# One shifted projection for q, k and v, and a token-ordered ring for transposed q and k

## The chip, the cores and the metric

The kernel runs on one core of a Trainium2 chip. The metric is the device time of one execution in microseconds, lower being better; the figure for the kernel before is the median of three runs. Traces come from a hardware profiler, one execution per trace. Engine names are those of the profile: PE multiplies matrices (PEld is its weight loading), DVE is the vector engine, ACT the scalar engine, POOL the GpSimd engine, SP the queue that issues all DMAs of this kernel.

## What is computed

One encoder block over 2048 tokens of width 1024, in float32: an RMS norm, one wide input projection, two attention mixers, SiLU and sigmoid gates, and two further projections. The change lies in the attention part:

```python
q = rms_norm(q.reshape(bsz, S, H, 64), gain) * scale      # per head, k likewise
# mixer A: 8 query heads on 2 key heads, |key - query| <= 128, with a sink logit
# mixer B: three groups of 8 heads, offsets dilation*j with |j| <= 64, dilation 1, 4, 16
logits = where(valid, q @ k.T + bias_table[t5_bucket(rel * dilation)], -1e30)
out = softmax(logits) @ v     # the three groups of B are then joined by their denominators
```

A dilation of d splits the tokens into d classes (token modulo d); each class of 2048/d tokens attends within itself. So dilation 1 has one class of 16 blocks of 128 tokens, dilation 4 has four classes of 4 blocks, dilation 16 has sixteen classes of one block.

## The kernel before

The input is normed, transposed and kept in SBUF as two fp16 halves, `XH` and `XL` (high part and remainder), features on partitions and tokens along the free axis, with the first 256 tokens repeated behind the last. A product in near-float32 precision is three fp16 products: high by high, high by low, low by high.

After a start of about 80 us the main stage projects and attends in 14 **units** (`UNITS`): two of kind A (4 query heads and one key head each) and twelve of kind B (2 heads of one dilation). Counted from 0, units 4, 7, 10 and 13 are of dilation 1, units 1, 5, 8 and 11 of dilation 4; these eight are called **shifted** (`un.shift`). Every unit has 16 blocks of 128 tokens, worked in 8 pairs (`class Pair`). From about 1400 us on come the merge gates, the branch projections and the output projection.

Steps of one pair, in order:

- `matmuls` (L651): 24 steps (8 feature chunks by 3 fp16 products) with the token block as weights and the weight columns streamed, into a PSUM tile `pj` of 384 columns (q, k, v).
- `evac_qk`, `v_hi`, `v_lo` (L670, L685, L691): out of PSUM. `v_ones` (L678) is a small POOL memset of a v tile.
- `square`, `stats`, `newton`, `scale`, `gain`, `hi`, `lo`, `swap`: the per-head norm and the split into fp16 halves `spl`. `newton` is twelve small POOL instructions (L270 to L273), `gain` POOL L722, `swap` POOL L737.
- `turn` (L745): one DMA transpose for each block from `spl` into a tile `kq` of 6 rows of 128 tokens (q heads, then k halves).

An `Item` is one query block with two heads. `logits` (L805) multiplies q against the keys, `maxima` adds the bias and takes the row maximum on DVE, `exps`, `hi`, `lo` make two fp16 halves of the probabilities, `turn` (L843) transposes them by DMA, `values` (L854) multiplies with v. In dilation-1 units two POOL steps join the three groups: `collect` (L989) and `products` (L1010).

In a shifted unit a query block of 128 tokens needs 64 tokens of keys on either side. So k and v are projected from token blocks shifted by 64 (block c holds tokens 128c-64 to 128c+63; block 0 wraps around), and the keys of query block i are the shifted blocks i and i+1. Before, q is projected from unshifted blocks: two accumulations for each token block, 24 matmuls of 128 columns (q) and 24 of 256 (k and v), each with its own weight load. `kq` tiles come from 6 rotating buffers, with 3 more (`kq0`) for block 0, which the last item needs again. Each segment of keys from one tile takes two matmuls of its own (`v` = 0, 1) for each head.

**What sets the order.** Nothing is scheduled by a planner. `at(t, f)` puts a step at a position t on a common clock whose unit is one pair; `until(t)` emits all steps due. `NORM`, `LAGS`, `LS` and others hold the offsets. The time of emission alone sets the place in each engine's queue, and each engine works its queue strictly in that order; a step that waits holds up all that stand behind it. The logits of a pair's first item stand 2.887 after the pair's begin (`LS`); `turn` stands 1.118 after the pair's last projection. `FILLS` lists pairs in which gate projections are streamed as well; units 10 and 13 have none.

Of the kernel before, what the change touches and what calls it, by code (L numbers as in the profile page):

```python
# [101 lines left out]
T_OUT = (0.1, 0.1, 1.431, 2.0)  # L102
FILLS = ((2, None, (2, 2, 4, 5)), (3, 0, (8, 9, 10, 12)), (4, 1, (17, 18, 20, 21)), (5, 2, (24, 25, 26, 28)), (6, 3, (32, 35, 37, 38)), (7, 4, (40, 41, 42, 44)), (9, 6, (57, 59, 60, 61)), (10, 7, (64, 65, 66, 68)), (11, 10, (88, 89, 90, 92)), (8, 13, (116, 116, 118, 118)))
XT_BUFS = 14
KQ_BUFS = 6
VT_BUFS = 10
PT_BUFS = 4
N_BIAS_A = 384
# [3 lines left out]
def block_kernel(tc, x, w_units, w_gate, w_mrg, w_brn, w_out, w_bra, gain, qkg, sink, bias_a, bias_b, b_merge, out):  # L112
# [514 lines left out]

        return min(t, NPAIR + 1 + DRAIN * (t - NPAIR - 1))

    def subset(X, g, r, c, aligned):  # L630
        o = 128 * c if aligned else (128 * c or S // DIL[g]) - 64
        return xclass((XH, XL)[X], g, r)[:, :, o:o + 128]

    class Pair:

# [6 lines left out]
        def matmuls(self, i):  # L642
            un, (r, c) = self.un, self.subsets[i]
            self.ps[i] = ps = pj_p.tile([128, 512], F32, name="pj")
            out = []
            for a, b, aligned in ((0, 128, True), (128, 384, False)) if un.shift else ((0, 384, True),):
                h, lo = subset(0, un.g, r, c, aligned), subset(1, un.g, r, c, aligned)
                k = 0
                for ch in range(NCH):
                    for lhs, rhs in ((h, un.wh), (h, un.wl), (lo, un.wh)):  # L650
                        out.append(lambda lhs=lhs, rhs=rhs, ch=ch, a=a, b=b, k=k: T.matmul(  # L651
                            ps[:, a:b], lhsT=lhs[:, ch, :], rhs=rhs[:, ch, a:b], start=(k == 0), stop=(k == 23)))
                        k += 1
            return out

        def plan(self, e):
# [80 lines left out]
                G.tensor_copy(sp[:, i, nh:, :, :], sp[:, i, nq:nh, ::-1, :])  # L737

        def turn(self):
            for i, s in enumerate(self.subsets):  # L740
                if self.un.shift and s[1] == 0:
                    kq = wk.tile([128, 6, 128], F16, name="kq0", bufs=3)
                else:
                    kq = wk.tile([128, 6, 128], F16, name="kq", bufs=KQ_BUFS)
                nc.sync.dma_start_transpose(out=kq[:], in_=self.sp[:, i].rearrange("p a b c -> p (a b c)"))  # L745
                self.un.kq[s] = kq


    class Item:
        def __init__(self, un, r, i, h0):  # L750
            self.un, self.r, self.i, self.h0 = un, r, i, h0
            n = un.n
            self.p0 = 0
            if un.kind == "A":
                cs = [c for c in (i - 1, i, i + 1) if 0 <= c < n]
                self.keys = [((0, c), 0, 128) for c in cs]
                self.b0 = 128 * (cs[0] - i + 1)
            elif n == 1:
                cs = [0]
                self.keys = [((r, 0), 0, 128)]  # L760
                self.b0 = 64
            else:
                cs = [i, (i + 1) % n]
                self.keys = [((r, i), 0 if i else 64, 128), ((r, (i + 1) % n), 0, 128 if i + 1 < n else 64)]
# [24 lines left out]

        def logits(self):  # L790
            un = self.un
            q = un.kq[(self.r, self.i)]
            if un.kind == "A":
                self.sv = [s_p.tile([128, 512], F32, name="s")[:, :self.W] for _ in range(2)]
            else:
# [2 lines left out]
            for j in range(2):  # L798
                h = self.h0 + j
                kh = 0 if un.kind == "A" else h  # L800
                o = 0
                for s, k0, k1 in self.keys:
                    kt = un.kq[s]
                    for v in range(2):
                        T.matmul(self.sv[j][:, o:o + k1 - k0], lhsT=q[:, h, :],  # L805
                                 rhs=kt[:, un.nq + kh + v * un.nk, k0:k1], start=(v == 0), stop=(v == 1))
                    o += k1 - k0

# [938 lines left out]
```

## Time and profile before

| | us |
|---|---|
| median of 3 runs (lowest, highest) | 1958.43 (1956.13, 1965.45) |
| span of the profiled execution, first to last instruction | 1958.6 |
| busy in the span: PE, DVE, ACT, POOL | 1935.7, 1377.4, 1059.8, 956.0 |
| 0 to 80 us: PE busy | 71.1 of 80 |
| 80 to 480, 480 to 880, 880 to 1280 us: PE busy of 400 | 399.5, 397.0, 396.1 |
| 1400 to 1958 us: PE busy of 558 | 554.0 |

The profile gives no time of the profiled execution other than its span, which is 0.2 us from the median.

How to read what follows: an engine's row of busy time adds up the union of its instructions. Matmuls overlap each other in the record, so what a matmul costs in a stream is the distance between two starts, not its length. In the list of waits a row names who waited, for whom, how long in total, how often, and the longest. In the timeline a row has start, length, engine, line, operation and tiles; the idle time before it stands in brackets if there was any.

### The profile page before, as it was taken

The numbers are of one execution on the slowest core, as the hardware profiler recorded it, in microseconds if no ns is written. First come the engines' busy times: TensorE is split into PE (matmuls) and PEld (weight loads), VectorE is DVE, ScalarE is ACT, GpSimd is POOL, SyncE is SP. The second block draws the span as 40 slices with busy tenths as digits, with TensorE's granted clock in tenths as the row PEclk, the third lists the DMA queues.
The fourth block names the chain that finished last, engine by engine and source line by source line (L and its number), as shares of the span: only waits on it lengthen the run. The fifth ranks groups of instructions, "written<-read, shape, count | busy, mean of one in ns | idle before, by whom it ended". The sixth has DMA issues, their size and how long they took to land.

```text
span 1958.6 us, 48091 instructions
## 1 busy us (share of the span) xinstructions
PE 1935.7 (99%) x17606; PEld 1392.0 (71%) x17606; DVE 1377.4 (70%) x3604; ACT 1059.8 (54%) x2415; POOL 956.0 (49%) x2440
## 2 busy tenths in 40 slices
PE   8999999999999999999999999999999999999999
PEld 5567896677788898888989889899544444444444
DVE  6668777888768776667876878767776757876312
ACT  7457656776565566565666655656534545432100
POOL 4254556455546656647566676656511210232533
PEclk8999999999999999999999999999999999999999
DMA  6239987797848596677777776755822346788763
GB/s 250 81 81 168 194 150 159 141 187 141 177 101 184 118 185 126 125 148 164 152 132 154 135 169 126 143 118 118 187 81 85 106 165 195 218 241 268 252 228 145
DMA packets 589773, 308.46 MB, mean 157 GB/s; under 512 B 458080, under 2 KB 527328, under 8 KB 588256
## 3 DMA queue, kind: packets, MB, share of 16 engines
q1 hardware_dynamic: 589536, 305.39, 67.0%
q8 instruction: 137, 2.24, 0.5%
q14 instruction: 100, 0.82, 0.1%
HBM read 129.91 MB, written 65.27 MB: 100 GB/s over the span
## 4 chain that ended last, share of the span: by engine, by line
PE 80%; DVE 6%; POOL 6%; issue 4%; ACT 2%; DMA 2%; SPq 0%; POOLq 0%; DVEq 0%; ACTq 0%
PE pj L651 32%; PE pj L308 14%; PE fps L308 13%; PE fps L1614 7%; PE fps L1409 5%; PE s L805 4%; PE pv L854 4%; POOL rs_t L270 1%; DVE rw L715 1%; POOL rs_t L271 1%; DVE qss L703 1%; POOL rs_t L272 1%; POOL rw L722 1%; POOL rs_y L273 1%; PE pt L916 1%
## 5 line engine op out<-in xcount | busy, mean ns | idle before, releaser
L651 PE MATMUL pj<-wl,XH 128*128 128x128 f16 (+2 forms) x2816 | 715.2, 268 | 0.0
L651 PE MATMUL pj<-wh,XH 128*128 128x128 f16 (+2 forms) x2816 | 708.7, 268 | 4.0 <-DVE vt L691 4.0
L651 PE MATMUL pj<-wh,XL 128*128 128x128 f16 (+2 forms) x2816 | 711.6, 269 | 0.0
L651 PEld LDWEIGHTS <-XH 128*128 128x128 f16 x5632 | 574.6, 113 | 64.7 <-issue 5.8
L651 PEld LDWEIGHTS <-XL 128*128 128x128 f16 x2816 | 318.1, 113 | 26.7 <-issue 0.5
L820 DVE CUSTOM_DVE_ANT_0 pr<-s,b,ubuf 128x256 f32<-128x256 f32 (+3 forms) x512 | 218.6, 464 | 48.6 <-PE s L805 47.0
L270 POOL TENSOR_TENSOR rs_t<-rs_y 128x8 f32<-128x8 f32 (+2 forms) x345 | 105.4, 306 | 207.5 <-DVE rs_y L261 142.7
L837 DVE SCALAR_TENSOR_TENSOR p<-pr,p 128x512 f16<-128x512 f32 (+2 forms) x256 | 185.0, 723 | 21.6 <-ACT p L833 21.1
L308 PEld LDWEIGHTS <-wh 128*128 128x128 f16 x960 | 93.7, 98 | 111.0 <-issue 1.5
L715 DVE TENSOR_TENSOR rw<-rw,qr 128x512 f32<-128x512 f32 (+1 forms) x112 | 111.6, 997 | 86.7 <-POOL vt L678 58.4
L722 POOL TENSOR_TENSOR rw<-rw,g 128x128 f32<-128x128 f32 (+1 forms) x224 | 131.1, 605 | 78.1 <-DVE rw L715 62.1
L833 ACT ACTIVATE p<-pr 128x512 f16<-128x512 f32 (+2 forms) x256 | 159.5, 623 | 7.1 <-issue 0.3
L670 ACT ACTIVATE rw<-pj 128x256 f32<-128x256 f32 (+1 forms) x224 | 86.5, 386 | 134.3 <-PE pj L651 133.4
L737 POOL COPY spl<-spl 128x256 f16<-128x256 f16 (+1 forms) x224 | 93.7, 448 | 127.2 <-DVE spl L732 125.7
L308 PE MATMUL fps<-Y,wh 128*128 128x512 f16 x512 | 152.2, 379 | 0.0
L805 PE MATMUL s<-kq 128*128 128x128 f16 (+1 forms) x1856 | 147.3, 218 | 1.5 <-DMA kq<-spl 1.4
L805 PEld LDWEIGHTS <-kq 128*128 128x128 f16 x2016 | 129.8, 98 | 25.1 <-issue 2.0
L308 PE MATMUL pj<-XH,gh 128*128 128x512 f16 x384 | 145.5, 379 | 0.0
L308 PE MATMUL pj<-XH,gl 128*128 128x512 f16 x384 | 145.5, 379 | 0.0
L308 PE MATMUL pj<-XL,gh 128*128 128x512 f16 x384 | 145.5, 379 | 0.0
L1614 PE MATMUL fps<-wt,M 128*128 128x512 f16 (+1 forms) x684 | 145.2, 375 | 0.0
L728 ACT ACTIVATE spl<-rw 128x512 f16<-128x512 f32 (+1 forms) x112 | 72.1, 644 | 126.2 <-POOL vt L678 87.0
(241 smaller groups left out, 3702.2 us busy)
## 6 DMA issues: line engine op xcount, KB each, us to landing
wraw<-in_w_units_dram SPq DMA_DIRECT2D x56, 384.0 KB, 4.6
mtd<-mm SPq DMA_DIRECT2D x56, 256.0 KB, 3.7
M<-mtd SPq DMA_DIRECT2D x8, 1792.0 KB, 9.5
mgd<-fg SPq DMA_DIRECT2D x39, 256.0 KB, 2.1
zd<-z SPq DMA_DIRECT2D x128, 66.0 KB, 1.9
zz<-zd SPq DMA_DIRECT2D x64, 132.0 KB, 2.9
xt<-in_x_dram SPq DMA_DIRECT2D x16, 512.0 KB, 8.9
gtd<-yo SPq DMA_DIRECT2D x32, 256.0 KB, 2.7
```

The source lines that it names most:

```text
L270: G.tensor_tensor(tv, yv, yv, OP.mult)
L308: out.append(lambda w=w, xx=xx, ch=ch, i=i: T.matmul(ps[:], lhsT=w[:, ch, c0:c0 + 128], rhs=xx[:, ch, ts], start=(i == 0), stop=(i == n - 1)))
L651: out.append(lambda lhs=lhs, rhs=rhs, ch=ch, a=a, b=b, k=k: T.matmul(ps[:, a:b], lhsT=lhs[:, ch, :], rhs=rhs[:, ch, a:b], start=(k == 0), ...
L715: V.tensor_tensor(q, q, self.rr[:, :n].unsqueeze(2).to_broadcast([128, n, HD]), OP.mult)
L722: G.tensor_tensor(q[:, i, :un.nq, :], q[:, i, :un.nq, :], g, OP.mult)
L737: G.tensor_copy(sp[:, i, nh:, :, :], sp[:, i, nq:nh, ::-1, :])
L805: T.matmul(self.sv[j][:, o:o + k1 - k0], lhsT=q[:, h, :], rhs=kt[:, un.nq + kh + v * un.nk, k0:k1], start=(v == 0), stop=(v == 1))
L820: V.tensor_tensor_reduce(out=self.pv[:, j, self.p0:self.p0 + W], in0=self.sv[j], in1=un.bias[:, self.h0 + j, self.b0:self.b0 + W], scale=I ...
L833: A.activation(self.sp[:, :128 * n], self.pr, AF.Copy, scale=PSC)
L837: V.scalar_tensor_tensor(self.sp[:, 128 * n:], self.pr, PSC, self.sp[:, :128 * n], OP.mult, OP.subtract)
L1409: mm.append(lambda ch=ch, k=k, w=w, i=i: T.matmul(ps[:], lhsT=weight(bl, ch)[w], rhs=xblock(x, ch)[k], start=(i == 0), stop=(i == 11)))
L1614: mm.append(lambda ch=ch, k=k, w=w, i=i: T.matmul(ps[:, :cols.stop - cols.start], lhsT=m[:, a, ch, k, :], rhs=wt[w][:, b, ch, cols], start ...
```

## The change

In shifted units q is projected from the same shifted blocks as k and v, in one accumulation of 24 matmuls with 384 columns. Query block i then lies half in shifted block i and half in block i+1.

To make it one operand, `kq` becomes a single tile, a ring of two halves. Each half has room for four blocks in token order (512) and an edge of 64. `turn` writes the blocks one after another into the ring, for all units, A and dilation 16 too. Where a query block spans the end of a half, the 64 tokens behind it are copied to the edge of that half by a new POOL step, `edge`, put 0.45 (`KQ_COPY`) after `turn` for each block whose number is a multiple of 4. In dilation 4 this is one copy of 6 rows for each class (16 in all), which also serves as the wrapped block. In dilation 1 it is one copy of 6 rows at block 0 into a small tile `kq0`, copies of the 2 q rows at blocks 4, 8 and 12, and one more of 2 rows at block 12 (20 in all). `logits` joins neighbouring segments of keys that lie in a row into one matmul of up to 384 keys.

```diff
-KQ_BUFS = 6
+RING = 576
+KQ_COPY = 0.45
...
-    def subset(X, g, r, c, aligned):
-        o = 128 * c if aligned else (128 * c or S // DIL[g]) - 64
-        return xclass((XH, XL)[X], g, r)[:, :, o:o + 128]
+    def subset(X, un, r, c):
+        o = (128 * c or S // un.d) - 64 if un.shift else 128 * c
+        return xclass((XH, XL)[X], un.g, r)[:, :, o:o + 128]
+
+    ring = wk.tile([128, 6, 2 * RING], F16, name="kq", bufs=1)
+    blocks = [0]
...
-            for a, b, aligned in ((0, 128, True), (128, 384, False)) if un.shift else ((0, 384, True),):
-                h, lo = subset(0, un.g, r, c, aligned), subset(1, un.g, r, c, aligned)
-                k = 0
-                for ch in range(NCH):
-                    for lhs, rhs in ((h, un.wh), (h, un.wl), (lo, un.wh)):
-                        out.append(lambda lhs=lhs, rhs=rhs, ch=ch, a=a, b=b, k=k: T.matmul(
-                            ps[:, a:b], lhsT=lhs[:, ch, :], rhs=rhs[:, ch, a:b], start=(k == 0), stop=(k == 23)))
-                        k += 1
+            h, lo = subset(0, un, r, c), subset(1, un, r, c)
+            for ch in range(NCH):
+                for lhs, rhs in ((h, un.wh), (h, un.wl), (lo, un.wh)):
+                    k = len(out)
+                    out.append(lambda lhs=lhs, rhs=rhs, ch=ch, k=k: T.matmul(
+                        ps[:, :384], lhsT=lhs[:, ch, :], rhs=rhs[:, ch, :], start=(k == 0), stop=(k == 23)))
...
         def turn(self):
-            for i, s in enumerate(self.subsets):
-                if self.un.shift and s[1] == 0:
-                    kq = wk.tile([128, 6, 128], F16, name="kq0", bufs=3)
-                else:
-                    kq = wk.tile([128, 6, 128], F16, name="kq", bufs=KQ_BUFS)
-                nc.sync.dma_start_transpose(out=kq[:], in_=self.sp[:, i].rearrange("p a b c -> p (a b c)"))
-                self.un.kq[s] = kq
+            un = self.un
+            for i, (r, c) in enumerate(self.subsets):
+                k = blocks[0] % 8
+                blocks[0] += 1
+                o = RING * (k // 4) + 128 * (k % 4)
+                nc.sync.dma_start_transpose(out=ring[:, :, o:o + 128], in_=self.sp[:, i].rearrange("p a b c -> p (a b c)"))
+                un.kq[r, c] = ring, o
+                if un.shift and c % 4 == 0:
+                    at(now[0] + KQ_COPY, self.edge, r, c, o)
+
+        def edge(self, r, c, o):
+            un = self.un
+            if c:
+                e = RING * (o < RING) + 512
+                G.tensor_copy(ring[:, :un.nq, e:e + 64], ring[:, :un.nq, o:o + 64])
+            elif un.n == 4:
+                G.tensor_copy(ring[:, :, o + 512:o + 576], ring[:, :, o:o + 64])
+                un.kq[r, 4] = ring, o + 512
+            else:
+                first = wk.tile([128, 6, 64], F16, name="kq0", bufs=1)
+                G.tensor_copy(first[:], ring[:, :, o:o + 64])
+                un.kq[r, un.n] = first, 0
+            if c and c + 4 == un.n:
+                G.tensor_copy(ring[:, :un.nq, o + 512:o + 576], un.kq[r, un.n][0][:, :un.nq, :])
...
-            q = un.kq[(self.r, self.i)]
+            q, qo = un.kq[self.r, self.i]
+            qo += 64 if un.shift else 0
+            runs = []
+            for s, k0, k1 in self.keys:
+                kt, o = un.kq[s]
+                if runs and runs[-1][0] is kt and runs[-1][2] == o + k0:
+                    runs[-1][2] = o + k1
+                else:
+                    runs.append([kt, o + k0, o + k1])
...
-                for s, k0, k1 in self.keys:
-                    kt = un.kq[s]
+                for kt, k0, k1 in runs:
                     for v in range(2):
-                        T.matmul(self.sv[j][:, o:o + k1 - k0], lhsT=q[:, h, :],
+                        T.matmul(self.sv[j][:, o:o + k1 - k0], lhsT=q[:, h, qo:qo + 128],
                                  rhs=kt[:, un.nq + kh + v * un.nk, k0:k1], start=(v == 0), stop=(v == 1))
```

Line numbers move by up to 27: L651 becomes L654, L805 becomes L832, the copies of `edge` are L757, L759, L763 and L766. In the built programs the orders of ACT and DVE are the same as before, SP issues the same DMAs in the same order, and POOL has 36 more instructions, all of them these copies. The projections of shifted units go from 6144 matmuls to 3072, the logits from 2016 to 1184, with as many columns in all.

POOL in unit 10 at block 8, before. `vt` is a v tile, `zz` the joined groups, `rw` q and k in the norm, `wraw` the weights of the next unit:

```order
L273 TENSOR_TENSOR qr_20537<-rs_t_20538,rs_y_20491 128x8 [waits Pool_49]
L1010 TENSOR_TENSOR zz_20270<-zz_20270,bm_e_20401 128x4x64 [waits DVE_49,Activation_49]
L1010 TENSOR_TENSOR zz_20270<-zz_20270,bm_e_20401 128x4x64 [waits DMAHW2_49,DVE_49]
L1010 TENSOR_TENSOR zz_20270<-zz_20270,bm_e_20401 128x4x64 [waits DMAHW3_49,DVE_49]
L678 MEMSET vt_20575 128x2 [waits PE_49]
L989 COPY zz_20495<-nmB_19225 128x4
L722 TENSOR_TENSOR rw_20354<-rw_20354,g1_874 128x128 [waits DVE_49]
```

The same place now:

```order
L274 TENSOR_TENSOR qr_17480<-rs_t_17481,rs_y_17442 128x8 [waits Pool_49]
L1037 TENSOR_TENSOR zz_17278<-zz_17278,bm_e_17378 128x4x64 [waits DVE_49,Activation_49]
L1037 TENSOR_TENSOR zz_17278<-zz_17278,bm_e_17378 128x4x64 [waits DMAHW2_49,DVE_49]
L1037 TENSOR_TENSOR zz_17278<-zz_17278,bm_e_17378 128x4x64 [waits DMAHW3_49,DVE_49]
L680 MEMSET vt_17509 128x2 [waits PE_49]
L757 COPY kq_1001<-kq_1001 128x2x64 [waits DMAHW0_49]
L1016 COPY zz_17445<-nmB_16502 128x4
L724 TENSOR_TENSOR rw_17341<-rw_17341,g1_874 128x128 [waits DVE_49]
```

The copy stands behind the twelve Newton steps, the three products and a memset, and waits for the transpose of block 8; the gain of the next pair stands behind it.

PE at the logits of item 7 of the same unit, before (`pj` is the projection, `s` the logits):

```order
L651 MATMUL pj_20586<-wl_18275,XH_80 128x256
L805 LDWEIGHTS kq_20259
L805 MATMUL s_20666<-kq_20259 128x128
L805 LDWEIGHTS kq_20259
L805 MATMUL s_20666<-kq_20259 128x128
L805 LDWEIGHTS kq_20259
L805 MATMUL s_20666<-kq_20482,kq_20259 128x128 [waits DMAHW0_49]
```

And now:

```order
L654 MATMUL pj_17516<-wh_15571,XH_80 128x384
L832 LDWEIGHTS kq_1001 [waits Pool_49]
L832 MATMUL s_17578<-kq_1001 128x128
L832 LDWEIGHTS kq_1001
L832 MATMUL s_17578<-kq_1001 128x128
L832 LDWEIGHTS kq_1001
L832 MATMUL s_17578<-kq_1001 128x128 [waits DMAHW0_49]
```

The query operand now spans the edge, so its first weight load waits for POOL's copy, where before only the third matmul waited, for a transpose.

More of the change, by code (lines that the diff above doesn't have):

```diff
@@ L763, in __init__ @@
                 cs = [i, (i + 1) % n]
-                self.keys = [((r, i), 0 if i else 64, 128), ((r, (i + 1) % n), 0, 128 if i + 1 < n else 64)]
+                self.keys = [((r, i), 0 if i else 64, 128), ((r, i + 1), 0, 128 if i + 1 < n else 64)]
                 self.b0 = self.p0 = 0 if i else 64
```

## The prediction

> **What bounds the kernel now.** I read the busy times and the chain of waits first, then the windows of the projection stage, then the distances between matmul starts, and last POOL's and PE's timelines where the new copies stand.
>
> ```profile
> PE 1935.7 (99%) x17606; PEld 1392.0 (71%) x17606; DVE 1377.4 (70%) x3604; ACT 1059.8 (54%) x2415; POOL 956.0 (49%) x2440
> PE 80%; DVE 6%; POOL 6%; issue 4%; ACT 2%; DMA 2%; SPq 0%; POOLq 0%; DVEq 0%; ACTq 0%
> PE pj L651 32%; PE pj L308 14%; PE fps L308 13%; PE fps L1614 7%; PE fps L1409 5%; PE s L805 4%; PE pv L854 4%; POOL rs_t L270 1%; DVE rw L715 1%; POOL rs_t L271 1%; DVE qss L703 1%; POOL rs_t L272 1%; POOL rw L722 1%; POOL rs_y L273 1%; PE pt L916 1%
> ```
>
> PE is busy 99% of the span and holds 80% of the chain, and the projection that is changed (L651) is its largest part. Does PE ever stand still where the change is?
>
> ```profile
> 206.00:300.00 94.00, 93.86 (x1242) 83.78 (x1240) 74.42 (x204) 59.81 (x141) 48.53 (x134) 1.00 0.88 162
> 1060.00:1145.00 85.00, 81.10 (x1036) 73.19 (x1033) 67.95 (x200) 52.67 (x138) 57.16 (x170) 0.98 0.78 154
> 1311.00:1395.00 84.00, 82.80 (x1013) 69.79 (x1011) 65.64 (x197) 50.78 (x136) 54.02 (x164) 1.00 0.67 136
> ```
>
> The windows give sum, PE, PEld, DVE, ACT and POOL busy, granted clock, DMA share and GB/s. In unit 1 (first row) PE is idle for 0.1 us of 94. Only unit 10 (second row, 3.9 us) and unit 13 (1.2 us) show idle time: they stream no gate projection, so what they wait for has least time there. So PE's own work sets the time, and a change pays by what it takes from PE's stream, unless it makes PE wait.
>
> **What the merged matmuls save.** PE streams as many columns as before; only the number of matmuls falls. What one costs beside its columns is read from distances between starts in runs without a break.
>
> ```profile
> 603.78 0.22 PE L651 MATMUL pj<-wh,XH 128*128 128x128 f16 x1
> ...
> 604.89 0.22 PE L651 MATMUL pj<-wh,XL 128*128 128x128 f16 x1
> 1111.67 0.27 PE L651 MATMUL pj<-wh,XH 128*128 128x256 f16 x1
> ...
> 1113.09 0.27 PE L651 MATMUL pj<-wl,XH 128*128 128x256 f16 x1
> 721.69 0.33 PE L651 MATMUL pj<-wh,XL 128*128 128x384 f16 x1
> ...
> 722.99 0.33 PE L651 MATMUL pj<-wl,XH 128*128 128x384 f16 x1
> L651 PE MATMUL pj<-wh,XL 128*128 128x128 f16 x1024 | 184.1, 219 | 0.0
> L651 PE MATMUL pj<-wh,XL 128*128 128x256 f16 x1024 | 279.4, 273 | 0.0
> L651 PEld LDWEIGHTS <-XH x5632: 95/113/207, 80.4 to 1375.7; 128*128 128x128 f16 x195
> ```
>
> Rows 1 to 21 of the 128-column run take 1.11 us: 55.5 ns each. The 14 rows of 256 columns: 1.42/13 = 109.2 ns. The 9 rows of 384: 1.30/8 = 162.5 ns. A pair of 128 and 256 thus costs 164.7, the merged one 162.5: 2.2 ns less, with a reading error of about 0.7. The 219 and 273 ns of the grouped rows are lengths of overlapping matmuls; whoever subtracts those gains some 160 ns that do not exist. I take 2.4 ns. 1024 pairs for each of three operand pairs are 3072: 3072 x 2.4 = **7.4 us**. The logits lose 832 matmuls in the same way: **2.0 us**. Bounds for the sum of 9.4: 3904 x 1.7 = 6.6 and x 2.9 = 11.3. The weight loads that go (113 ns by median) lie beside the stream, since a 128-column matmul follows the last after 55.5 ns with a load of its own.
>
> The Trainium skill ("TensorE: Matmul & The Clock Gate", Back-to-back issue gap) says that in a stream of load and matmul the spacing is set by both, about 81 ns at 128 columns and 131 at 512. By the trace it is 55.5 at 128, so here its formula for the isolated gap (columns over 2.4 plus 2.5 ns) agrees and the sustained figures do not. By those figures the saving would be near 60 ns a pair, an estimate.
>
> **What the copies cost on POOL.** 36 copies; nearest rows:
>
> ```profile
> L737 POOL COPY spl<-spl 128x256 f16<-128x256 f16 x192 | 80.0, 446 | 109.1 <-DVE spl L732 107.6 <-DVE ubuf L1138 1.5
> L737 POOL COPY spl<-spl 128x128 f16<-128x128 f16 x32 | 13.7, 459 | 18.1 <-DVE spl L732 18.1
> ```
>
> The copies of 2 rows are 128 elements: 0.46 us; those of 6 rows are 384, say 0.6. About 19 us in all on an engine that is half idle; it costs only where something waits behind it or for it. Behind it: the copy waits for its transpose, and POOL's queue with it. The worst place is unit 1:
>
> ```profile
> 276.42 2.71 SPq L745 DMA_TRANSPOSE kq<-spl  x2
> 278.92 0.65 POOL L270 TENSOR_TENSOR rs_t<-rs_y 128x8 f32<-128x8 f32 x1 [2.66 <-DVE rs_y L261]
> DMA to landing us min/median/max: 6.3/6.7/7.0
> ```
>
> Landing 7.0 us after 276.4 (usual: 2.9), plus 0.6, the copy ends at 284.0, and the Newton steps behind it start 5 us late. Their idle time before later DVE results takes most of that back; the transpose they lead to is at most 2 us late. Price 0 to 2 us, I take 0.6. In other places the copy either finds its data landed or fits into such a gap.
>
> **Who waits for the copies.** In dilation 4 an edge is read one pair later. In dilation 1 the copies at blocks 4, 8 and 12 are read at once, by items 3, 7 and 11: twelve places. In each I take the end of the POOL instruction that the copy will follow and the start of the logits on PE. Units 10 (blocks 4, 8), 13 (blocks 8, 12), and as a contrast 7 (block 12):
>
> ```profile
> 1094.66 0.11 POOL L678 MEMSET vt<- 128x2 f16 x1
> 1094.25 0.49 PE L805 MATMUL s<-kq 128*128 128x128 f16 x6 [0.29 <-DMA kq<-spl]
> 1117.20 0.10 POOL L678 MEMSET vt<- 128x2 f16 x1
> 1113.20 0.91 PE L805 MATMUL s<-kq 128*128 128x128 f16 x8
> 1365.36 0.10 POOL L678 MEMSET vt<- 128x2 f16 x1
> 1363.28 0.61 PE L805 MATMUL s<-kq 128*128 128x128 f16 x8
> 1387.78 2.20 POOL L1010 TENSOR_TENSOR zz<-zz,bm_e 128x256 f32<-128x256 f32 x3
> 1387.39 0.61 PE L805 MATMUL s<-kq 128*128 128x128 f16 x8
> 890.70 0.10 POOL L678 MEMSET vt<- 128x2 f16 x1
> 892.35 0.61 PE L805 MATMUL s<-kq 128*128 128x128 f16 x8
> ```
>
> With 0.46 for the copy, PE waits 1095.23 - 1094.25 = 1.0; 1117.76 - 1113.20 = 4.6; 1365.92 - 1363.28 = 2.6; 1390.44 - 1387.39 = 3.1: **11.3 us**. In unit 7 the copy would end 1.1 us before it is wanted. Of the other seven places six have that or more by the same reading, and block 4 of unit 13 has about nothing to spare. So POOL, out of the way until now, comes to hold up PE in the two units without filling.
>
> A pause of PE has an after-effect:
>
> ```profile
> 512.60:516.10 3.50, 3.50 (x13) 1.88 (x12) 2.71 (x15) 2.31 (x8) 0.44 (x2) 0.51 1.10 259
> 1123.60:1127.10 3.50, 3.33 (x29) 2.90 (x30) 2.48 (x12) 3.21 (x11) 2.59 (x12) 0.51 0.76 154
> PE pj L651 <- DVE vt L691: 2.8, 2, 2.4
> PE s L805 <- DMA kq<-spl: 0.8, 1, 0.8
> PE pj L651 <- DVE vt L691: 0.8, 1, 0.8
> ```
>
> Both windows follow the longest pauses behind the start, and in both the granted clock is 0.51 for 3.5 us: 1.7 us lost. The three longer waits would add 3 x 1.7 = **5.1**. Against that, other engines catch up while PE stands: the waits of unit 10 (2.8, with one slow window of 1.7) and of unit 13 (0.8 and 0.8) come behind the new pauses and can go: **-6.1**. In unit 13 POOL is behind PE by less once PE has paused at block 8, so the wait at block 12 (3.1, and its slow window 1.7) may shrink; I take off 2.1 of these 4.8.
>
> Sum: -9.4 + 11.3 + 5.1 - 6.1 - 2.1 + 0.6 = -0.6, on a span of 1958.6 that lies 0.2 above the median. I forecast **1958 us**, no change. Its own range: the low saving and half of the relief, 1958.6 - 6.6 + 11.3 + 5.1 + 0.6 - 4.1 = 1965; the high saving, all of the relief and no slow windows, 1958.6 - 11.3 + 11.3 + 0.6 - 8.2 = 1951.
>
> **Rivals.** *The copies hide.* If POOL reaches them earlier, or PE later (the logits now stand behind a different share of the projection, a few tenths of a us), no pause arises: 1958.6 - 9.4 = 1949, and 1946 if half of the old 5.1 us of idle time goes too. For it: eight of twelve places have room. Against: 4.6 us is more than a shift of tenths removes.
>
> *POOL becomes the bound of dilation-1 units.* Price: pauses 11.3, slow windows 5.1, nothing given back since DVE's and POOL's lag follows PE's results, 3 us more where the copy delays the next pair's gain and transpose, and four more places of some 2 us in units 4 and 7: 1958.6 - 9.4 + 11.3 + 5.1 + 3 + 8 = 1977. It is slower than before from the point where pauses exceed 9.4 us in all. For it: POOL's queue runs several us behind PE in units 10 and 13. Against: units 4 and 7 have fillings and slack.
>
> *Transposes into a tile with gaps are slower.* No row shows one; the rows are 2.9 us for `kq` and 3.6 for the larger `pt`:
>
> ```profile
> pt<-p SPq DMA_TRANSPOSE x256, 3.6
> kq<-spl SPq DMA_TRANSPOSE x224, 2.9
> ```
>
> At 0.7 us more, the 16 pairs of units 10 and 13 would each be late by that, 11 us on top of the forecast: 1969. Against: the packets are the same rows of `spl`, and only the place of each block changes. The Trainium skill ("DMA: Bandwidth & Descriptors", Latency and other measured facts) gives a loss of about 30% for a transpose whose middle dimension is not contiguous; on 2.9 us that is 0.9, an estimate.
>
> *Weight loads bind after all.* If a 128-column matmul lasted as long as its load, 113 instead of 55.5 ns, 3072 x 57.5 = 177 us would go: 1782. The starts speak against it. The sustained figures of the Trainium skill weighed above would be of this kind.
>
> **How the numbers follow.** Chances: the forecast 0.58, copies hide 0.16, POOL bound 0.17, slower transposes 0.07, weight loads 0.02. About 0.5% (9.8 us) is what a measurement of this kernel can tell from no change. Faster than that is reached only by hidden copies with some idle time gone, or by weight loads: 0.18. Slower: POOL or transposes, 0.24. Within: 0.58. The range of 8 in 10 runs from hidden copies with idle time gone, 1947, to short of the full POOL case, 1974.
>
> **What would show it.** The saving: starts of the shifted projection 162.5 ns apart, L651's successor without rows of 128 and 256 columns. The pauses: a new row in PE's list of waits, logits waiting for POOL, near 11 us, in units 10 and 13 and none in 4 and 7; windows of clock 0.5 behind them. The relief: PE's waits for L691's successor below 1 us. The forecast is wrong if that row is under 3 us (then 1949) or over 20, or if the transposes' median rises by more than 0.3 us.

## The result, and the profile after

| | median (lowest to highest), us | runs | profiled span, us |
|---|---|---|---|
| before | 1959.77 (1956.13 to 1965.45) | 20 | 1958.6 |
| after | 1956.16 (1953.14 to 1959.52) | 20 | 1956.9 |

The ratio after to before is 0.9979, with a 95% interval of 0.9972 to 0.9986: 4.1 us less (2.7 to 5.5). That is a gain clear of zero, but one within the 0.5% that the prediction counts as no change. Some 3900 matmuls are gone, worth 9.4 us by the prediction's working. Some 5 us of that came back as something else. The execution profiled after is one of the slower of its 20 (1958.90 us at a mean granted clock of 0.994; the ten fastest have 0.996 or 0.997), and the two profiles lie only 1.7 us apart.

The page of the kernel after: first the busy times, then the chain of waits by engine.

```profile
PE 1926.9 (98%) x13702; PEld 1213.0 (62%) x13702; DVE 1377.4 (70%) x3604; ACT 1063.0 (54%) x2415; POOL 971.2 (50%) x2476
PE 82%; POOL 6%; DVE 5%; issue 3%; DMA 2%; ACT 1%; SPq 0%; POOLq 0%; DVEq 0%; ACTq 0%
```

PE is busy 8.8 us less (1935.7 before), but the span is only 1.7 shorter. So PE stands idle for 30.0 us where it was 22.9. The windows around units 1, 10 and 13 say where, with the columns as in the prediction.

```profile
206.00:300.00 94.00, 92.42 (x837) 65.44 (x836) 74.17 (x201) 59.22 (x140) 49.26 (x135) 1.00 0.82 161
1060.00:1145.00 85.00, 78.72 (x624) 51.23 (x621) 68.75 (x200) 51.82 (x131) 60.39 (x175) 0.98 0.74 148
1311.00:1395.00 84.00, 78.31 (x604) 47.80 (x603) 65.22 (x198) 49.04 (x126) 56.76 (x162) 0.98 0.67 135
```

In unit 10 (second row) PE is idle for 6.3 us in place of 3.9, in unit 13 (third) for 5.7 in place of 1.2. PE's waits, grouped by what is waited for (us in total, times, longest):

```profile
PE s L832 <- POOL kq L757: 11.1, 5, 3.8
PE pt L195 <- DVE yo L947: 3.4, 2, 1.8
PE pj L654 <- DVE vt L693: 1.7, 3, 0.9
```

The first row is new: the logits wait for POOL's copy of an edge. The last one, VectorE's release of a projection tile, and the wait of the logits for their transposes stood like this in the same view of the kernel before:

```profile
PE pj L651 <- DVE vt L691: 4.0, 4, 2.4
PE s L805 <- DMA kq<-spl: 1.4, 3, 0.8
```

4.0 became 1.7, and the 1.4 have no row left. The middle row was one wait of 3.0 before; now it is two, of 1.58 at 291.3 us and 1.84 at 511.2 us. Here is PE's timeline of the kernel after (start, length, then in brackets how long PE stood before the row, and for whom), at the five places of the first row, cut from several stretches:

```profile
1090.50 0.62 PE L832 MATMUL s<-kq 128*128 128x128 f16 x8 [1.58 <-POOL kq L757]
1113.26 0.50 PE L832 MATMUL s<-kq 128*128 128x128 f16 x3 [3.79 <-POOL kq L757]
1338.98 0.62 PE L832 MATMUL s<-kq 128*128 128x128 f16 x8 [0.56 <-POOL kq L757]
1360.77 0.62 PE L832 MATMUL s<-kq 128*128 128x128 f16 x8 [2.81 <-POOL kq L757]
1384.93 0.56 PE L832 MATMUL s<-kq 128*128 128x128 f16 x7 [2.31 <-POOL kq L757]
```

They are blocks 4 and 8 of unit 10 and blocks 4, 8 and 12 of unit 13. The longest one, seen from POOL in the same kernel:

```profile
1110.12 2.65 POOL L1037 TENSOR_TENSOR zz<-zz,bm_e 128x256 f32<-128x256 f32 x3
1112.72 0.10 POOL L680 MEMSET vt<- 128x2 f16 x1
1112.76 0.45 POOL L757 COPY kq<-kq 128x128 f16<-128x128 f16 x1
```

PE stands from 1109.47 on. The copy itself takes 0.45 us; it starts at 1112.76 because POOL is still at work on the three products that join the groups (L1037), which stand ahead of it. This pause is the queue ahead of the copy, not the copy. The one at 1090.50 is only in part: with the edges written by transposes (below) PE still waits 1.04 us there, for the transpose.

Windows of 3.5 us of the kernel after, at the places behind the start where the clock was low in either kernel (the number after the five engines is the granted clock):

```profile
512.20:515.70 3.50, 3.50 (x15) 2.19 (x13) 2.56 (x15) 1.75 (x6) 1.25 (x5) 0.53 1.27 212
1113.00:1116.50 3.50, 3.24 (x16) 2.04 (x17) 3.33 (x10) 1.20 (x4) 3.37 (x7) 0.52 1.15 254
1123.60:1127.10 3.50, 3.50 (x24) 2.40 (x23) 3.19 (x14) 3.19 (x7) 2.38 (x7) 1.00 0.98 141
1386.20:1389.70 3.50, 3.50 (x10) 1.25 (x9) 2.29 (x8) 2.75 (x6) 0.98 (x3) 0.51 1.13 307
```

Three low windows in place of two: the one at 1123.6 is gone, and those at 1113 and 1386 stand at the ends of new pauses. The pause of 2.81 at 1360.8 left none, while the one of 1.84 at 511.2 has the window at 512.

The saving itself, in PE's timeline of the kernel after (first and last of 8 matmuls without a break):

```profile
532.79 0.33 PE L654 MATMUL pj<-wh,XH 128*128 128x384 f16 x1
...
533.93 0.33 PE L654 MATMUL pj<-wl,XH 128*128 128x384 f16 x1
```

1.14/7 = 163 ns from start to start, as forecast. From the first projection matmul of a unit to that of the next, units 4, 5, 7 and 8 are shorter by 1.10, 1.11, 0.96 and 0.60 us; 16 blocks x 24 matmuls x 2.4 ns are 0.92 of it and the joined logits the rest; in unit 8 a new wait of 0.47 us takes part of it back. Units 10 and 13 are longer by 1.24 (to the next unit's start) and 1.13 (to the last projection), and unit 11 is 1.72 shorter, an old wait of 0.42 near its start being gone as well.

### The profile page after: what moved, and what is told of

Read it like the earlier page. It is cut to its first block, busy times and chain, and to the rows that moved or that the text cites. A ratio compares the mean times of both kernels' runs of the same rounds, so it can differ in the third digit from the quotient of the medians.

```text
span 1956.9 us, 40345 instructions
## 1 busy us (share of the span) xinstructions
PE 1926.9 (98%) x13702; PEld 1213.0 (62%) x13702; DVE 1377.4 (70%) x3604; ACT 1063.0 (54%) x2415; POOL 971.2 (50%) x2476
## 4 chain that ended last, share of the span: by engine, by line
PE 82%; POOL 6%; DVE 5%; issue 3%; DMA 2%; ACT 1%; SPq 0%; POOLq 0%; DVEq 0%; ACTq 0%
PE pj L654 33%; PE pj L309 14%; PE fps L309 13%; PE fps L1641 7%; PE fps L1436 5%; PE s L832 4%; PE pv L881 4%; POOL rs_t L271 1%; POOL rs_t L272 1%; DVE qss L705 1%; POOL rs_t L273 1%; DVE rw L717 1%; POOL rw L724 1%; DMA kq<-spl 1%; POOL rs_y L274 1%
## 5 line engine op out<-in xcount | busy, mean ns | idle before, releaser
L654 PE MATMUL pj<-wh,XL 128*128 128x384 f16 x1792 | 587.2, 328 | 0.0
L654 PE MATMUL pj<-wh,XH 128*128 128x384 f16 x1792 | 585.3, 327 | 1.7 <-DVE vt L693 1.7
L654 PE MATMUL pj<-wl,XH 128*128 128x384 f16 x1792 | 585.9, 327 | 0.0
L654 PEld LDWEIGHTS <-XH 128*128 128x128 f16 x3584 | 413.2, 117 | 150.9 <-issue 3.9
L654 PEld LDWEIGHTS <-XL 128*128 128x128 f16 x1792 | 207.9, 116 | 69.2 <-issue 0.7
L832 PE MATMUL s<-kq 128*128 128x256 f16 (+3 forms) x1168 | 148.3, 255 | 11.1 <-POOL kq L757 11.1
L881 PEld LDWEIGHTS <-pt 128*128 128x128 f16 x3024 | 125.7, 97 | 35.0 <-issue 0.2
```

What stands on the lines that cost most here:

```text
L654: out.append(lambda lhs=lhs, rhs=rhs, ch=ch, k=k: T.matmul(ps[:, :384], lhsT=lhs[:, ch, :], rhs=rhs[:, ch, :], start=(k == 0), stop=(k == ...
L832: T.matmul(self.sv[j][:, o:o + k1 - k0], lhsT=q[:, h, qo:qo + 128], rhs=kt[:, un.nq + kh + v * un.nk, k0:k1], start=(v == 0), stop=(v == 1))
L881: T.matmul(self.po[:, j, :w], lhsT=p[:, n * j + s, :], rhs=un.v[key][:, vh, c0:c0 + w], start=(k == 0 and s == 0), stop=(k == 2 and s == n ...
```

## The experiments

All were compared with the kernel before on the same chip, in 5 rounds, the projection in three parts in 3 rounds. The chips differ, and the kernel before took 1958.23 to 1960.21 us on them, so kernels are compared by their ratios. The third column is what PE lost around units 10 and 13: the sum of its pauses of 0.2 us and more between 1045 and 1400 us of the profiled execution.

| kernel | median, us | PE's pauses there, us | ratio (95%) |
|---|---|---|---|
| before | - | 5.6 | 1 |
| after | 1956.16 | 12.0 | 0.9979 (0.9972 to 0.9986) |
| merged projection alone | 1953.25 | 8.2 | 0.9973 (0.9958 to 0.9988) |
| no edges in dilation 1 | 1952.46 | 9.2 | 0.9967 (0.9954 to 0.9979) |
| edges by a second transpose | 1953.23 | 10.3 | 0.9970 (0.9960 to 0.9980) |
| the same, less VectorE work | 1945.91 | 4.8 | 0.9935 (0.9917 to 0.9953) |

### The merged projection alone

On the kernel before; ring, joined logits and copies are left away.

```diff
-            for a, b, aligned in ((0, 128, True), (128, 384, False)) if un.shift else ((0, 384, True),):
-                h, lo = subset(0, un.g, r, c, aligned), subset(1, un.g, r, c, aligned)
+            h, lo = subset(0, un, r, c), subset(1, un, r, c)
...
-                            ps[:, a:b], lhsT=lhs[:, ch, :], rhs=rhs[:, ch, a:b], start=(k == 0), stop=(k == 23)))
+                        ps[:, :384], lhsT=lhs[:, ch, :], rhs=rhs[:, ch, :], start=(k == 0), stop=(k == 23)))
```

> The kernel before with the merged projection alone: kq tiles, their buffers and the logits stay as they were, no ring, no copies. The queries of shifted units then come from tokens 64 earlier than they should. Theory (each merged matmul saves its fixed cost of about 2.4 ns and nothing else changes): 3072 x 2.4 = 7.4 us less than before, ratio 0.9962, near 1952, no logits waiting for POOL, waits of units 10 and 13 much as before (4 to 6 us). Rival (the ring and its dependences cost something, or the projection saves less than its starts say): under 4 us less than before.

1953.25 us against 1958.63: 5.3 us less (2.4 to 8.2), with the priced 7.4 inside. The waits are not as before:

```profile
PE pj L650 <- DVE vt L689: 6.3, 6, 2.8
PE s L803 <- DMA kq<-spl: 1.9, 2, 1.1
```

There is no copy in this kernel, and still PE waits longer than before: 6.3 us for VectorE's release of a projection tile (4.0 before). A shorter projection alone already brings PE to that release earlier than VectorE does.

### The segments not joined

```diff
-                if runs and runs[-1][0] is kt and runs[-1][2] == o + k0:
+                if False:
```

> The changed kernel with a matmul for each segment of keys, as before the change, instead of joined segments: 832 more matmuls in the logits. Theory (fixed cost alone): 832 x 2.4 = 2 us more than the changed kernel, near 1958, logits of 8 matmuls at the same lengths, pauses as they are. Rival (fewer matmuls pay by shorter waits of DVE for the logits too, or the joined ones bring nothing): over 4 us more, or none.

1959.66 us, ratio 0.9997 (0.9988 to 1.0007): 0.18% or 3.5 us behind the change. The two intervals leave 0.4 to 6.9; the priced 2.0 lies inside, but so does part of the rival's range, and the run does not decide.

### The projection in three parts

```diff
-            for ch in range(NCH):
...
-                        ps[:, :384], lhsT=lhs[:, ch, :], rhs=rhs[:, ch, :], start=(k == 0), stop=(k == 23)))
+            for a, b in ((0, 128), (128, 256), (256, 384)) if un.shift else ((0, 384),):
...
+                            ps[:, a:b], lhsT=lhs[:, ch, :], rhs=rhs[:, ch, a:b], start=(k == 0), stop=(k == 23)))
```

> The changed kernel with the projection of shifted units in three accumulations of 128 columns (q, k, v apart, all from the shifted block) instead of one of 384: 6144 more matmuls, all else as changed. Theory (each matmul costs a fixed 2.2 to 2.4 ns beside its columns): starts 55.5 to 55.8 apart, 3072 x (3 x 55.7 - 162.5) = 3072 x 4.6 = 14 us, less some us where units 10 and 13 wait less: 1964 to 1970. Rival (a 128-column matmul lasts as long as its weight load, 113 ns): over 500 us more.

1969.31 us, ratio 1.0049 (1.0030 to 1.0068). Against the change that is 0.70%, 13.7 us for 6144 more matmuls: 2.2 ns each (1.4 to 3.1 by the ends of the two intervals). PE waits less in this kernel, though: 7.5 us for the copies and 0.4 for VectorE's release, 4.9 less than in the change. Added to the 13.7 that would make 3.0 ns each. Units 4, 5 and 7, which have no such waits, are 2.04, 2.07 and 1.83 us longer for 768 more matmuls, 2.4 to 2.7 ns each. By these three readings the price is 2.2 to 3.0 ns, and the 2.4 taken lies inside. If a 128-column matmul had to last as long as its weight load, three of them would have cost 3072 x (3 x 113 - 162.5) ns = 542 us; that rival falls.

### No edges in dilation 1

```diff
-                e = RING * (o < RING) + 512
-                G.tensor_copy(ring[:, :un.nq, e:e + 64], ring[:, :un.nq, o:o + 64])
+                pass
...
-            qo += 64 if un.shift else 0
```

> The changed kernel without the copies at blocks 4, 8 and 12 of dilation-1 units (16 of 36 go), and with queries of shifted units read from the block itself instead of 64 tokens on, so that no query operand spans an edge; instruction counts on PE are the same. Theory (the 11.1 us of pauses behind POOL's copies are lost time): no logits waiting for POOL, 7 to 11 us less than the changed kernel, 1945 to 1949. Rival (units 10 and 13 are bound by the chain through DVE and POOL, and the pauses only stand where other waits would): the waits for vt and kq grow to 6 us or more, and the time is 1952 or above.

1952.46 us, ratio 0.9967 (0.9954 to 0.9979). The 11.1 us of waiting for POOL are gone, and only some 2.4 us of time went with them, with overlapping intervals. That is the rival's outcome. Its waits:

```profile
PE pj L654 <- DVE vt L693: 8.8, 7, 3.0
```

The rows of the kernel after were 11.1 (POOL) and 1.7 (VectorE); now it is 0 and 8.8. The idle time moved to another releaser. So most of the time in the pauses behind the copies would have been spent on another wait.

### The copies earlier in POOL's queue

```diff
-                    at(now[0] + KQ_COPY, self.edge, r, c, o)
+                    at(now[0] + (0.20 if c else KQ_COPY), self.edge, r, c, o)
```

> The changed kernel with the copies at blocks 4, 8 and 12 put 0.20 instead of 0.45 behind turn: they stand ahead of the Newton steps of the next pair on POOL. Theory: POOL then waits for the transpose to land (about 3 us from the end of swap) with the Newton steps behind it; logits no longer wait for POOL by more than 1 us each, but the next pair's transpose is 2 to 3 us later, and in units 10 and 13 part of the pauses comes back as logits or projection waiting for DMA or DVE: 1949 to 1955. Rival (POOL has time to spare there): as without edges, 1945 to 1949.

1962.83 us, ratio 1.0025 (1.0015 to 1.0036): slower than the change, where both outcomes written down were faster. Its waits:

```profile
PE pj L654 <- DVE vt L693: 15.6, 8, 4.8
PE s L832 <- POOL kq L757: 0.8, 2, 0.5
```

PE hardly waits for the copy any more. But the copy now stands in POOL's queue ahead of the Newton steps and waits there for its transpose: POOL stands idle 33.5 us ahead of the twelve copies, where it was 4.2. What comes out of POOL later makes VectorE late (at block 8 of unit 10 it waits 3.54 us for the Newton result, 1.06 in the change), and PE waits for VectorE 15.6 us. An early place in a queue is no gain for an instruction whose own input comes late.

### The edge by a second transpose

SyncE transposes 64 tokens of `spl` a second time, to the edge's place, in `turn`; of POOL's copies at blocks 4, 8 and 12 only that of the wrapped block at 12 is left.

```diff
+                if un.shift and c and c % 4 == 0:
+                    e = RING * (o < RING) + 512
+                    nc.sync.dma_start_transpose(out=ring[:, :un.nq, e:e + 64],
+                                                in_=self.sp[:64, i, :un.nq].rearrange("p a b c -> p (a b c)"))
...
-                G.tensor_copy(ring[:, :un.nq, e:e + 64], ring[:, :un.nq, o:o + 64])
+                pass
```

> The changed kernel with the edge at blocks 4, 8 and 12 written by a second, small DMA transpose of 64 tokens straight from spl, issued by SP behind the block's own transpose; POOL copies nothing there but the wrapped block at 12. The result is complete. Theory: the edge lands about 1 us behind its block, before PE wants it, so the pauses go as in the run without edges, and the 12 small transposes cost SP about 1 us each where its queue has room: 1946 to 1951. Rival (what is queued behind on SP, the transposes of the probabilities, is late for PE): values wait for DMA, 1953 or above.

1953.23 us, ratio 0.9970 (0.9960 to 0.9980). It is clearly faster than before; whether it beats the change stays open, since the intervals overlap. The time is the rival's, but not for the rival's reason: the values do not wait for DMA. The waits are those of the kernel without edges, with 2.0 us for the transposes:

```profile
PE pj L654 <- DVE vt L693: 8.3, 6, 2.6
PE s L835 <- DMA kq<-spl: 2.0, 2, 1.0
```

What is VectorE doing while PE waits? Its timeline in this kernel, up to the release (L693) for which PE stood 2.56 us:

```profile
1109.43 1.08 DVE L717 TENSOR_TENSOR rw<-rw,qr 128x512 f32<-128x512 f32 x1 [1.06 <-POOL qr L274]
1110.43 1.10 DVE L867 SCALAR_TENSOR_TENSOR p<-pr,p 128x512 f16<-128x512 f32 x1
1111.45 0.83 DVE L1046 TENSOR_TENSOR ya<-zz 128x256 f32<-128x256 f32 x1
1112.39 0.64 DVE L1047 TENSOR_TENSOR ya<-ya,zz 128x256 f32<-128x256 f32 x1
1112.95 0.41 DVE L1022 TENSOR_TENSOR bm_n<-zz 128x4 f32<-128x4 f32 x1
1113.40 0.96 DVE L1023 TENSOR_TENSOR bm_n<-bm_n,zz 128x4 f32<-128x4 f32 x1
1114.39 1.02 DVE L1024 TENSOR_TENSOR bm_e<-bm_n,zz 128x12 f32<-128x12 f32 x1
...
1116.75 0.28 DVE L693 SCALAR_TENSOR_TENSOR vt<-pj,vt 128x128 f16<-128x128 f32 x1
```

From 1109.43 on no idle time stands in brackets: VectorE works without a break, among it the merge of the three groups for earlier pairs (L1022 to L1047), and the small instruction that releases PE's tile stands behind that in its queue. From 1060 to 1145 us VectorE is idle for a fifth (69.20 of 85 us busy in this kernel), yet here it is the one that is late.

### The merge later, and the fillings elsewhere

If the release is late because the merge stands ahead of it, does the merge do better a quarter pair later? And do units 10 and 13 do better with some of their neighbours' gate projections?

```diff
-B_MERGE = (-0.037, 0.133, 0.333, 0.507, 0.665, 1.053)
+B_MERGE = (-0.037, 0.403, 0.603, 0.777, 0.935, 1.323)
```

> The changed kernel with the steps that join the three groups in dilation-1 units (exponents to sums) put 0.27 of a pair later; all else as changed, the result complete. On POOL the copies at blocks 8 and 12 of units 10 and 13 then stand ahead of the three products (2.65 us) instead of behind them, and on DVE the release of PSUM stands ahead of the merge's small operations. Theory (the pauses are made by what stands ahead in the queues): logits waiting for POOL fall by about 2.6 us at each of three places, from 11 to 3 to 5 us, and waits for vt stay under 3: 1948 to 1952. Rival (the chain through DVE is as long whatever its order): waits for POOL fall, waits for vt rise by as much, 1954 to 1957.

1960.29 us, ratio 1.0007 (0.9999 to 1.0016), slower than either outcome. The waits of the change with this merge:

```profile
PE pj L654 <- DVE vt L693: 9.4, 10, 3.0
PE s L832 <- POOL kq L757: 4.6, 5, 1.5
PE fps L195 <- ACT wl L220: 2.8, 2, 2.5
```

The wait for POOL falls from 11.1 to 4.6, that for VectorE rises from 1.7 to 9.4, and the end of the kernel gets 2.5 us that were not there. The same merge with edges by transposes:

> The edge by a small transpose and the merge steps 0.27 of a pair later. Theory (the waits for vt in units 10 and 13, 7.5 us without copies, come from the merge's operations ahead of the release of PSUM in DVE's queue): those waits fall below 3 us and the time to 1946 to 1950, below the run with the small transpose alone. Rival (DVE has too much work there in any order): waits for vt of 6 us or more, 1952 to 1955 as with the small transpose alone.

1961.09 us, ratio 1.0005 (0.9996 to 1.0015), slower than either outcome. PE waits 10.0 us for L693 (8.3 with the merge in its old place). A row of VectorE's timeline, 2.5 us ahead of a release for which PE stood 2.74 us:

```profile
1114.25 0.85 DVE L734 TENSOR_TENSOR spl<-rw,spl 128x512 f16<-128x512 f32 x1 [1.31 <-ACT spl L730]
```

So here VectorE does not work without a break: an instruction ahead of the release waits 1.31 us for ACT, and of the merge only the two sums (L1046, L1047) still stand between. The release hangs on a chain through the other engines as well as on VectorE's own work. And in the kernel before, as a control:

> The kernel before with the merge steps 0.27 of a pair later, as a control. Theory: its waits for vt (4.0 us, with a slow window) mostly go, 1954 to 1957, so that against an equally placed merge the change is worth 6 to 9 us, near the fixed cost of its matmuls. Rival: no difference to before, 1958 to 1960.

1963.92 us, ratio 1.0030 (1.0019 to 1.0041). That too is slower than either outcome. So the later merge costs every one of the three about 0.3%, and the change keeps its 0.2% beside it. About 2 us of these 6 stand behind the units: one wait of PE for ACT (2.5 us, between 1463 and 1472), which is 0.4 or 0.5 in the three kernels without the later merge. The fillings, in the change:

```diff
-(10, 7, (64, 65, 66, 68)), (11, 10, (88, 89, 90, 92))
+(10, 7, (64, 66, 82, 84)), (11, 10, (88, 90, 106, 108))
```

> The changed kernel with four of the eight gate projections of units 8 and 11 moved into units 10 and 13 (two each, 5.2 us of PE work apiece); the result is complete. Theory (in units 10 and 13 PE has too little work for each pair, so POOL's copies and DVE's release of PSUM come late): POOL's copies cost PE under 4 us instead of 11, waits for vt stay under 3, units 8 and 11 have the room: 1945 to 1950. Rival (DVE's queue is as full in units 8 and 11, so the waits only move there): waits for vt of 5 us or more in units 8 and 11, 1953 or above.

1968.45 us, ratio 1.0039 (1.0024 to 1.0053). Its waits:

```profile
PE pj L654 <- DVE vt L693: 7.6, 6, 2.4
PE pt L943 <- DVE ya L1044: 4.9, 3, 2.9
PE s L832 <- POOL kq L757: 3.2, 1, 3.2
```

The longest waits for VectorE now stand in units 8 and 11, from which PE work was taken (those for L693 at 941, 1132 and 1195 us, those for L1044 at 952 and 1205). With transposed edges the same:

> Both: the edge by a small transpose as in the run with that alone, and the four gate projections moved. Theory: no waits over 1 us in units 10 and 13, 1943 to 1948, the full saving of the merged matmuls of 9 us and the old idle time besides. Rival (waits move to units 8 and 11): 1951 or above.

1961.76 us, ratio 1.0011 (1.0001 to 1.0021), with 7.7 us for L693 in the same places. These units have no slack to lend; both runs end as their rivals said.

### Less work in VectorE's queue

The runs that moved instructions moved waits. This one takes work out of VectorE's queue, in the kernel with transposed edges.

```diff
-            V.tensor_tensor(mn[:], mn[:], nm[:, 2], OP.min)
...
-            A.activation(e[:], e[:], AF.Exp)
+            A.activation(e[:, :2], e[:, :2], AF.Exp)
...
-            V.tensor_tensor(sd[:], sd[:], ed[:, 2], OP.add)
...
-            V.tensor_tensor(y, y, zz[:, 2, :, :, 0:HD], OP.add)
```

> The kernel with the transposed edges (no copies in dilation 1), and of the merge of the four key segments in units 4 to 14 three VectorE instructions per quarter of a unit left out: the third segment is missing from the minimum, from the sum of the denominators and from the sum of the outputs (and its factor is not put through the exponential). That is 222 + 229 + 487 ns = 0.94 us less in VectorE's queue, four times per unit, and nothing else. Theory (VectorE's queue in order, with the release of the projection's PSUM tile behind the merge, is what PE waits for in units 10 and 13 once POOL is out of the way): PE's waits for L693's release, 8.3 us in the kernel with all three, fall by up to 0.94 at each of the four places in these units, to 3 to 6 us; time 1947 to 1951 us, ratio about 0.995 to 0.9965. Rival (the release waits for something ahead of VectorE, ACT's copy of vt, POOL's products or a transfer, and VectorE's free time only moves idle time): the waits stay at 7 us or more and the time within 1 us of the kernel with all three, ratio 0.9965 to 0.9975.

1945.91 us, ratio 0.9935 (0.9917 to 0.9953): below the theory's range, and the rival falls. Its waits:

```profile
PE s L835 <- DMA kq<-spl: 2.8, 4, 1.2
PE pj L654 <- DVE vt L693: 1.5, 3, 0.8
```

L693's row falls from 8.3 to 1.5 us, more than the expected 0.94 at each of four places. The expectation had the number of merges wrong. It is the three groups that are merged, in the dilation-1 units, and this row of the kernel with transposed edges counts 32 merges, eight to a unit:

```profile
L1023 DVE TENSOR_TENSOR bm_n<-bm_n,zz 128x4 f32<-128x4 f32 x32 | 7.1, 222 | 1.1
```

Where the waits went fits the reading. Of the four in units 10 to 13 the one of 0.86 us at 1075.7, ahead of unit 10's first merge (1102 us), stays (0.84); those of 2.56, 2.37 and 1.85 at 1117.1, 1129.5 and 1365.5 are gone, and one of 0.29 stands at 1100.4. That what is spared early in a unit is spared again at its later waits was not tested apart.

Against the kernel with all three instructions it is 0.35% or 6.9 us. The pauses between 1045 and 1400 us are 5.5 less, and the low-clock window at 1129 us is gone, 1.7 more. In the profiled execution the window at 511 us is missing too; it stands ahead of the first merge of all (586 us), so the instructions left out cannot have removed it. The kernel before was not run with the same work left out, so how much of the 6.9 us it would have gained as well stays open.

## Why the prediction was right, and what was off

1958 us was forecast, in a range of 1947 to 1974, no change as the likeliest; 1956.16 was measured, a gain of 2.7 to 5.5 us that is smaller than what the prediction meant to tell from none. Step by step:

- **The merged matmuls, -7.4 and -2.0.** Right. The starts are 163 ns apart; three parts in place of one cost 2.2 to 3.0 ns a matmul, where 2.4 was taken; units 4, 5 and 7, without new waits, are 0.96 to 1.11 us shorter. The 2.0 for the logits was not fixed closer than 0.4 to 6.9.
- **The pauses behind POOL's copies, +11.3.** Right in place and size: 11.05 us by the five rows. Single places were off: block 4 of unit 10 took 1.58 (1.0 forecast), block 8 3.79 (4.6), unit 13's block 8 2.81 (2.6), its block 12 2.31 (3.1), and its block 4, with "nothing to spare", 0.56. That these cancel to within 0.3 us is luck. Units 4 and 7 have none, as said.
- **The relief, -6.1.** Right. Between 1045 and 1400 us PE's pauses other than for POOL fell from 5.6 to 0.9, and the low window at 1123.6 went: 6.4 in all. Over the whole kernel the wait for VectorE fell from 4.0 to 1.7, not below the 1 us that was given as a sign. The runs show the same from the other side: no edges, no pauses, and the wait for VectorE is at 8.8. This is why 11 us of new pauses cost only some 2.4 us against the kernel without edges: most of this time PE would have waited for VectorE a little later.
- **The low-clock windows, +5.1.** Too high. Three new ones were priced, and two came (1113 and 1386): 1.7 less. The pause at 1360.8 was the second longest and left none, so one window behind each of the long pauses, as the prediction took it, does not hold.
- **Unit 13's block 12, -2.1.** Too high. About 0.8 of it came (2.31 in place of 3.1); its low window was there. So this miss and that of the windows nearly cancel: 11.3 + 5.1 - 2.1 = 14.3 was priced, 11.05 + 2 x 1.7 = 14.5 came.
- **The late Newton steps in unit 1, +0.6.** A pause of 1.58 us stands at 291.3 in the kernel after, for VectorE. One of 0.90 stands there in the kernel with the merged projection alone, which has no copies; at most the rest can be the copies'. The copies' share was not isolated.
- **The copies in POOL's queue.** 19 us were reckoned in all; the rows of the kernel after sum to 19.2 (us in all, mean ns, then POOL's idle time before them):

```profile
L759 POOL COPY kq<-kq 128x384 f16<-128x384 f16 x16 | 10.4, 650 | 23.5 <-DMA kq<-spl 23.4
L757 POOL COPY kq<-kq 128x128 f16<-128x128 f16 x12 | 4.5, 379 | 4.2 <-DMA kq<-spl 4.2
L763 POOL COPY kq<-kq 128x384 f16<-128x384 f16 x4 | 2.9, 736 | 2.0 <-DMA kq<-spl 2.0
L766 POOL COPY kq<-kq 128x128 f16<-128x128 f16 x4 | 1.4, 342 | 0.0
```

POOL stands idle 30 us ahead of them for transposes. Outside the places named PE has no wait that is put down to a copy.

The sum came out at -0.6 and should have been near -4. The terms for units 10 and 13 fit the profile one by one, and the two profiles lie 1.7 us apart although the first unit starts 1.1 us later in the one after. The rest is open. The profiled execution after is 2.7 us above its median at a lower mean clock, so others may have fewer low windows; and a matmul price of 3.0 ns, the upper end above, would be 2.3 us more. Neither was tested.

Of the rivals, *copies hide* falls by the row of 11.1 us, and so does its time: with no pause for a copy (no edges) the kernel took 1952.46, not 1946 to 1949, since waits for VectorE's release took the place of the pauses. *POOL becomes the bound* had the right pauses, but nothing of its further price: the edges without POOL bring some 2 us. *Slower transposes* falls by the transposes of the kernel after:

```profile
kq<-spl SPq DMA_TRANSPOSE x224, 2.8
pt<-p SPq DMA_TRANSPOSE x256, 3.6
```

2.8 us where it was 2.9. The loss of about 30% that the Trainium skill ("DMA: Bandwidth & Descriptors", Latency and other measured facts) gives for a middle dimension that is not contiguous does not appear for these transposes, whose destination has the gaps. *Weight loads bind* falls by the run with three parts. By the sustained spacings of the Trainium skill ("TensorE: Matmul & The Clock Gate", Back-to-back issue gap), about 81 ns at 128 columns and 131 at 512, the three parts would have cost some 400 us in place of 13.7; this is an estimate (three times 81 ns in place of some 114 at 384 columns, read off between the two, 3072 times). The runs do not agree with them.

What the prediction did not say: once the projection is shorter, PE waits in units 10 and 13 for VectorE's release as soon as the copies are out of the way. In no run did the shorter projection alone bring the whole 9.4 us; 6.9 us more came when VectorE had less to do.

## What to carry to other kernels

Ask of every wait that an edit adds or removes what the waiting engine would wait for next: here 11 us of pauses cost some 2.4, and taking them away brought no more than that. Where waits only change their releaser as instructions are moved (six such runs were slower than the kernel they started from), look for less work on the path to the next releaser, however idle that engine is over the whole; 0.94 us less VectorE work per merge brought 6.9 us here. A small copy costs what stands ahead of it in its queue; another queue that has the data at hand can take that wait away, though here its gain in time is not clear of the noise.

## What the runs showed of the hardware

- Tiny VectorE instructions can take five times their usual time. L1023 and L1024 (4 and 12 elements a partition) took 0.96 and 1.02 us at 1113.4 and 1114.4 of the kernel with transposed edges, where L1023 has a mean of 222 ns. POOL then runs, almost to the same ends:

```profile
1113.31 1.03 POOL L325 TENSOR_TENSOR wraw<-wraw,gn 128x512 f32<-128x512 f32 x1
...
1114.34 1.03 POOL L325 TENSOR_TENSOR wraw<-wraw,gn 128x512 f32<-128x512 f32 x1
```

  The same pairs stand at 1361.8 and 1362.8 us of that kernel (0.96 and 1.02 us, beside 1.03 and 1.03). They stand side by side; that the one holds up the other was not tested.
- Copies of 128 elements on POOL took 0.29 us by median and up to 0.75 (12 of them), less than the 0.46 of the nearest row before.
- In the kernel after, pauses of 3.79, 2.31 and 1.84 us had a window of granted clock 0.5 that began between 0.2 us before their end and 1.3 us behind it; one of 2.81 had none. So the length alone does not decide it; what does stays open.
